# Layer 1's modulation blocks: scaled and added by GpSimd instead of multiplied by TensorE

## The chip, the cores and the metric

The kernel runs on one core of a Trainium2 chip. The time is device microseconds of one execution. A core has five engines with queues of their own: TensorE (PE; its weight loads are shown apart as PEld), VectorE (DVE), ScalarE (ACT), GpSimd (POOL) and SyncE (SP), which here only issues loads. SBUF is the on-chip memory; TensorE writes only to PSUM, which GpSimd does not touch here.

## The reference

Two models one after the other, on 256 tokens of width 1024. The change touches the first, which has two layers, and in them only the modulation ("adaln"): from a condition vector `c` each layer gets six vectors of 1024, which shift, scale and gate its two halves (mixer and experts).

```python
def adaln(cond, mod_w, mod_b):
    m = jax.nn.silu(cond) @ mod_w + mod_b        # (1024) @ (1024, 6144)
    return jnp.split(m, 6, axis=-1)
for i in range(2):
    sh1, sc1, g1, sh2, sc2, g2 = adaln(c, mod_w[i], mod_b[i])
    a = rms_norm(h, norm1_g[i]) * (1 + sc1) + sh1
    y = even_mixer(a, ...) if i == 0 else odd_mixer(a, ...)
    h = h + g1 * y
    h = h + g2 * hier_moe(modulate(h, norm2_g[i], sh2, sc2), ...)
```

Layer 0 also needs the first vectors of a second condition, `c_ctx`; layer 1 needs those of `c` alone. `hier_moe` routes each token to 2 of 16 experts, chosen within one of four groups. Everything is computed in float32.

## The kernel before

**Blocks.** A layer's modulation matrix is 24 MB, cut into 12 blocks of 512 output columns; a block is two loads of 1 MB (`chunk`, L125), each 128 partitions by four slices of 512. Block j of a layer gives columns 4j to 4j+3 of `mods[layer]` (48 columns of 128 values): 0 to 7 shift 1, 8 to 15 scale 1, 16 to 23 gate 1, 24 to 31 shift 2, 32 to 39 scale 2, 40 to 47 gate 2.

**How a block is computed.** The class `Conditions` (L357) does it on TensorE. `add` (L364) loads the two halves and multiplies each of the eight slices as the moving operand (128x512) with 32 columns of `cpad`, which holds silu(c) and silu(c_ctx) between zeros (L375); four slices stand in four strips of the array at one time, so the sum over partitions falls into four strips of one PSUM bank. `keep` copies the bank to SBUF on ScalarE (L384). `finish` multiplies the copy, in four pieces of 128 columns, with a selection matrix (L396), which adds the strips and turns the row into a column, and VectorE adds the bias (L399).

**Where the blocks stand.** The list `left` holds all 24 blocks in order, and `PLAN` (L58) says how many are taken at each of 17 places. Layer 0's are taken in its own mixer and do not concern the change. Layer 1's stand at four places:

- four (`PLAN[5]`) at the head of layer 0's experts (`moe`, L421), kept after the first gather and finished in step 1;
- two (`PLAN[16]`, the object `c3`, L1006) beside layer 1's value projection (`oin_v`);
- four (`PLAN[6]`, `more`, L404 and L1057) after the odd mixer's input projection, before its output projection;
- two (`PLAN[7]`) at the head of layer 1's experts.

**The experts' stage.** `moe` first computes the router on VectorE from the logits of the norm (L454 to L494): a chain of some thirty small instructions that ends in `selb`. TensorE then counts ranks (L483), VectorE makes one-hot matrices (`oh`, L513), and TensorE gathers the tokens of four experts (`gps`, L535) into `xg`. Eight steps follow (L748), two experts in each: `up` (L557), transposes (L571, L573), `down` (L590), and the scatter back (L599). The gather for the next four experts is made every second step (`prepare`). From step 2 the experts are taken in an order found at run time, so SP issues those loads (L717) only when VectorE has that order in memory. After step 7 stands a branch (L772) for experts with more than 64 tokens, which all engines take or skip; in this data it is taken once in layer 0 and skipped in layer 1.

**The odd mixer.** After a row norm, `oin_v` gives the value part (L1009), then eight chunks of the input projection (`feature_linear`, L201, called at L1039) follow, two for each of four parts, and four of the output projection (L1061). Each 1 MB chunk of these is split into two halves of 128x1024, and each half into a rounded part on ScalarE (`whi`, L133) and the remainder on VectorE (`wlo`, L134), with two buffers each; TensorE does three matmuls for each product. `Norm` (L228) begins, before the output projection, with matmuls on shift 2, and scale 2 goes into the gain it uses from the second chunk on.

**What sets the order.** Each engine runs its instructions in the order in which the program issues them, with small changes by the planner, and waits on semaphores. All 1 MB loads are issued by SP, in program order, each into the next of 13 buffers (three pools of 4, 7 and 2, `rings`, taken in turn); a load waits until what its buffer held has been used. So a load that waits holds up all loads behind it. PSUM has eight banks; tag "T" (`tps`) has two, one of which holds a fourth of the experts' result in that stage.

```python
T.matmul(self.ps[32 * k:32 * k + 32, :], cpad[:, 4 * h + k, 32 - 2 * at:64 - 2 * at],
         w[:, k, :], start=(at == 0 and h == 0), stop=(h == 1), tile_position=(0, 32 * k), ...)
```

Of the kernel before, what the change touches and what calls it, by code (L numbers as in the profile page):

```python
# [19 lines left out]
D = 1024  # L20
S = 256
# [31 lines left out]

GT = 9

FILL = (0, 0, 0, 1, 1, 2, 0, 2, 0)

PLAN = (1, 1, 1, 1, 2, 4, 4, 2, 1, 1, 0, 0, 0, 0, 0, 0, 2)  # L58


def build(tc, I, O):
# [3 lines left out]
    with es:  # L65
# [31 lines left out]
        def F(name):  # L97
            a, n = PF[name]
            return pf[:, a:a + n]
# [303 lines left out]

        def more(n, small):  # L404
            c = Conditions(small)
            c.add(n)
            c.finish()

# [11 lines left out]

        def moe(layer, norm, rc, work, blocks):  # L421
            small = work
            lg, shift = norm.lg, norm.router[1]
            cond = Conditions(work)
            cond.add(blocks)
            def t(n, name):
# [155 lines left out]
            def down(turned, dns, first, last):  # L582
                ht, back, cws = turned
                wd = [dns(e) for e in range(2)]
                yg = pair([128, D], "yg", small, bufs=2)
                for q in range(2):
# [37 lines left out]
            prepare(0)  # L624
            cond.keep()

# [121 lines left out]
            for step in range(9):  # L748
# [9 lines left out]
                if step < 8:  # L758
                    q, h_ = divmod(step, 2)
                    hs[step] = up(quarter[q][0], 128 * h_, lambda h, e: weights_of(step, h, e), turned)  # L760
                    if h_ == 0 and q < 3:
                        prepare(q + 1)
                    if step == 1:
                        rks, cws_, res = more_blocks()
                        cond.finish(kept=True)
                        V.tensor_copy(g2, mods[layer][:, 40:48, 0])
                else:
                    turned()
                    for e in range(2):
                        weights_of(7, 2, e)  # L770
                    over, rest = (value(intr, i, (EN.PE, EN.Activation, EN.DVE, EN.Pool), 8) for i in range(2))
                    with tc.If(over > 0):  # L772
                        overflow(res, cwp[:, :, 14:16], lambda h, e: weights_of(7, h, e), lambda e: weights_of(7, 2, e))
                        with tc.If(rest > 0):  # L774
                            overflow_any(0)
                            with tc.If(rest > 2):
                                for i in range(1, 4):
                                    overflow_any(i)
# [39 lines left out]
        with tc.tile_pool(name="l0", bufs=1) as wk:  # L818
# [158 lines left out]
            for cj in range(4):  # L977
# [3 lines left out]
                for mm in range(2):  # L981
                    m = 2 * cj + mm
                    residual(m, ps[:, S * mm:S * mm + S], mods[0][:, 16 + m:17 + m, 0])
                c2.add(PLAN[8 + cj])
            norm.add2(xT, 6)
            c2.finish()
            rc = norm.finish(after=AF.Exp, pool=c1)
        ring_m = b1.enter_context(tc.tile_pool(name="ring_m", bufs=2))
        rings[:] = [ring, ring_b, ring_b, ring_m, ring, ring_b, ring_b, ring, ring_b, ring_m, ring_b, ring, ring_b]
        with tc.tile_pool(name="m0", bufs=1) as wk:  # L990
            collect, norm = moe(0, norm, rc, wk, PLAN[5])
            for m in range(NK):
                collect(m)
                norm.add(xT, m)
            rx = norm.finish(c1)
# [4 lines left out]
        with tc.tile_pool(name="l1", bufs=1) as wk:  # L1000
# [4 lines left out]
            loaded["oin_v", 0] = chunk("oin_v", 0)  # L1005
            c3 = Conditions(wk, ops)  # L1006
            c3.add(PLAN[16])
            c3.keep()
            token_linear("oin_v", 0, (a,), lambda b, ps: A.copy(vt[:, b], ps.rearrange("p (g c) -> p g c", g=4)),  # L1009
                         need=step)  # L1010
            c3.finish(kept=True)
            vf = vt.rearrange("p b g c -> p (b g) c")
            sq = wk.tile([128, 8, 128], F32, name="vsq", tag="zc")
            A.activation(sq, vf, AF.Square)
# [6 lines left out]
            nc.scalar.dma_start(sgw, I["sg_w"])  # L1021
            sT = wk.tile([128, 4, S], F32, name="sT")
            for g in range(4):
# [10 lines left out]
            z = hx  # L1034
            zc = wk.tile([128, 4, S], F32, name="zc", tag="zc")
            cv = F("conv")
            for part in range(4):
                for cj in range(2):
                    ps = feature_linear("oin", 2 * part + cj, a)  # L1039
# [9 lines left out]
                    else:  # L1049
                        V.tensor_tensor(z[:, two], pv, hx[:, two], op=ALU.mult)  # L1050
                        for m in (2 * cj, 2 * cj + 1):
# [4 lines left out]
                                                   zc[:, m, 0:S - 1], op0=ALU.mult, op1=ALU.add)  # L1056
            more(PLAN[6], wk)  # L1057
            c2 = Conditions(wk, tps)
            norm = Norm(wk, None, router=(mod_gain(1, 4, 0, F("n2g")[:, 8:16], "G21"), mods[1][:, 24:32, 0], 1), tag=("mf", 2))
            for cj in range(4):  # L1060
# [3 lines left out]
                for mm in range(2):  # L1064
                    m = 2 * cj + mm
                    residual(m, ps[:, S * mm:S * mm + S], mods[1][:, 16 + m:17 + m, 0])
                c2.add(PLAN[12 + cj])
            norm.add2(xT, 6)
            c2.finish()
            rc = norm.finish(after=AF.Exp, pool=c1)  # L1070
        with tc.tile_pool(name="m1", bufs=1) as wk:
            collect, _ = moe(1, norm, rc, wk, PLAN[7])
        b1.close()
# [760 lines left out]
```

## Time and profile before

| | |
|---|---|
| Median of three runs | 1518.34 us (1518.15 to 1519.94) |
| Profiled execution | 1520.81 us, of which the span from first to last instruction is 1519.1 |
| TensorE busy | 1481.3 us, 98% of the span |
| VectorE busy | 858.3 us, 56% |
| ScalarE busy | 658.4 us, 43% |
| GpSimd busy | 28.5 us, 2%, 59 instructions |
| Mean granted TensorE clock | 0.981 of full speed |
| Data moved | 324.85 MB, 214 GB/s in the mean |

The first model fills some 615 us of the span: layer 0's mixer to about 170, its experts to 350, the odd mixer to 465, layer 1's experts to 617; the second model is not touched. A busy TensorE is not one at its peak, as matmuls are pipelined and their ends are modelled; the timeline tells more, where a row gives the start, the duration of a run of like instructions and, in brackets, the idle time before it with what ended that. The times in one execution differ from those of the median run by the 0.16% between 1520.81 and 1518.34.

### The profile page before, as it was taken

What the parts mean: (1) busy time and instruction counts of PE and PEld (TensorE: products, weight loads), DVE (VectorE), ACT (ScalarE), POOL (GpSimd) and SP (SyncE); (2) the same over time, 40 slices, a digit from 0 to 9 for tenths busy, and PEclk for the clock granted to TensorE, in tenths of its full rate; (3) what the DMA queues carried; (4) which work ended last, traced back from release to release, by engine and by line L of the source; (5) the groups of instructions that cost most, each with busy time, mean ns of one, the idle gap of its engine ahead of it and who ended that gap; (6) DMA issues with size and microseconds to landing.
All of it is one profiled execution on the core that took longest, in us unless ns stands there. A gap on an engine that the chain in (4) does not pass through costs nothing.

```text
span 1519.1 us, 25566 instructions
## 1 busy us (share of the span) xinstructions
PE 1481.3 (98%) x10410; PEld 1183.6 (78%) x10412; DVE 858.3 (56%) x1682; ACT 658.4 (43%) x1114; POOL 28.5 (2%) x59
## 2 busy tenths in 40 slices
PE   8999999989999999999999999999999999999998
PEld 3756644445985443698789999999898789999998
DVE  2775452225646221757777775555757777765554
ACT  2544311115433111565564554444564654654443
POOL 0000000000000000020000000000110000000000
PEclk9999899999999999999999999999999999999999
DMA  9974799739585985543315564554444134555540
GB/s 395 385 301 160 302 373 408 293 127 379 206 337 193 416 328 222 180 167 112 139 57 178 184 222 174 188 195 167 135 158 165 57 112 174 188 220 176 188 167 28
DMA packets 47005, 324.85 MB, mean 214 GB/s; under 512 B 5600, under 2 KB 5984, under 8 KB 8480
## 3 DMA queue, kind: packets, MB, share of 16 engines
q1 hardware_dynamic: 45360, 320.12, 55.4%
q8 instruction: 86, 1.41, 0.4%
q10 hardware_dynamic: 1296, 1.55, 0.3%
q0 software_dynamic: 224, 1.46, 0.3%
q14 instruction: 39, 0.32, 0.1%
HBM read 322.06 MB, written 1.05 MB: 213 GB/s over the span
## 4 chain that ended last, share of the span: by engine, by line
PE 55%; issue 3%; ACT 1%; DVE 1%; POOL 0%; DVEq 0%; POOLq 0%; ACTq 0%
PE fm L162 9%; PE fm L161 9%; PE fm L163 9%; PE d L162 4%; PE d L161 4%; PE d L163 4%; PE tm L194 1%; PE tm L196 1%; PE tm L195 1%; PE sp L1461 1%; PE lf L162 1%; PE lf L163 1%; PE lf L161 1%; PE po L1450 1%; PE ptp L1444 1%
## 5 line engine op out<-in xcount | busy, mean ns | idle before, releaser
L134 DVE TENSOR_TENSOR wlo<-w,whi 128x1024 fp32r<-128x1024 f32 (+1 forms) x314 | 378.4, 1208 | 254.2 <-ACT whi L133 251.6
L133 ACT CAST whi<-w 128x1024 fp32r<-128x1024 f32 (+1 forms) x314 | 324.4, 1035 | 393.6 <-PE fm L162 240.5
L161 PE MATMUL fm<-acth,whi 128*128 128x256 f32 x624 | 180.8, 290 | 0.0
L162 PE MATMUL fm<-actl,whi 128*128 128x256 f32 x624 | 179.9, 288 | 0.0
L163 PE MATMUL fm<-acth,wlo 128*128 128x256 f32 x624 | 179.1, 287 | 0.0
L163 PE MATMUL d<-hidh,wlo 128*128 128x256 f32 x512 | 144.2, 282 | 0.0
L162 PE MATMUL d<-hidl,whi 128*128 128x256 f32 x512 | 144.0, 281 | 0.0
L161 PE MATMUL d<-hidh,whi 128*128 128x256 f32 x512 | 143.9, 281 | 0.0
L162 PE MATMUL fm<-oTl,whi 128*128 128x256 f32 x512 | 143.6, 281 | 0.0
L163 PE MATMUL fm<-oTh,wlo 128*128 128x256 f32 x512 | 143.3, 280 | 0.0
L161 PE MATMUL fm<-oTh,whi 128*128 128x256 f32 x512 | 143.1, 280 | 0.0
L162 PEld LDWEIGHTS fm<-actl,whi 128*128 128x128 f32 x624 | 120.7, 193 | 3.2 <-issue 3.0
L163 PEld LDWEIGHTS fm<-acth,wlo 128*128 128x128 f32 x624 | 120.7, 193 | 2.2 <-issue 1.6
L161 PEld LDWEIGHTS fm<-acth,whi 128*128 128x128 f32 x624 | 121.4, 195 | 1.2 <-issue 0.8
L162 PEld LDWEIGHTS fm<-oTl,whi 128*128 128x128 f32 x512 | 96.8, 189 | 0.4 <-DVE oTl L1100 0.4
L162 PEld LDWEIGHTS d<-hidl,whi 128*128 128x128 f32 x512 | 96.7, 189 | 0.4 <-DVE hidl L134 0.4
L161 PEld LDWEIGHTS fm<-oTh,whi 128*128 128x128 f32 x512 | 96.9, 190 | 0.0
L161 PEld LDWEIGHTS d<-hidh,whi 128*128 128x128 f32 x512 | 96.8, 189 | 0.1
L163 PEld LDWEIGHTS d<-hidh,wlo 128*128 128x128 f32 x512 | 96.7, 189 | 0.1
L163 PEld LDWEIGHTS fm<-oTh,wlo 128*128 128x128 f32 x512 | 96.7, 189 | 0.0
L590 PE MATMUL yp<-w,ht 128*64 128x512 f32 x272 | 83.8, 643 | 6.9 <-PEq L774 3.5
L557 PE MATMUL gu<-w,xg 128*64 128x512 f32 x288 | 70.1, 599 | 0.0
(531 smaller groups left out, 2862.3 us busy)
## 6 DMA issues: line engine op xcount, KB each, us to landing
w<-gu SPq DMA_DIRECT2D x64, 1024.0 KB, 9.1
w<-mod SPq DMA_DIRECT2D x48, 1024.0 KB, 11.7
w<-dn SPq DMA_DIRECT2D x32, 1024.0 KB, 9.7
w<-gw SPq DMA_DIRECT2D x32, 1024.0 KB, 4.8
w<-up SPq DMA_DIRECT2D x32, 1024.0 KB, 4.8
w<-dw SPq DMA_DIRECT2D x32, 1024.0 KB, 4.8
w<-tm SPq DMA_DIRECT2D x12, 1024.0 KB, 4.8
w<-oin SPq DMA_DIRECT2D x8, 1024.0 KB, 8.2
```

The source lines that it names most:

```text
L133: A.copy(hi, src)
L134: V.tensor_sub(lo, src, hi.bitcast(F32))
L161: T.matmul(out, ws[0], xs[0], start=first, stop=False, skip_group_check=skip)
L162: T.matmul(out, ws[0], xs[1], start=False, stop=False, skip_group_check=skip)
L163: T.matmul(out, ws[1], xs[0], start=False, stop=last, skip_group_check=skip)
L194: T.matmul(ps, at[0], ww[0], start=first, stop=False, skip_group_check=True)
L195: T.matmul(ps, at[1], ww[0], start=False, stop=False, skip_group_check=True)
L196: T.matmul(ps, at[0], ww[1], start=False, stop=k == NK - 1, skip_group_check=True)
L557: T.matmul(gu[64 * e:64 * e + 64, :], x_[:, 4 * h + k, s0 + 64 * e:s0 + 64 * e + 64], w[e][:, 512 * k:512 * k + 512], start=(h == 0 and k ...
L590: T.matmul(yp[64 * e:64 * e + 64, :], ht[:, 128 * k + 64 * e:128 * k + 64 * e + 64], wd[e][:, 1024 * k + 512 * q:1024 * k + 512 * q + 512] ...
L1444: T.transpose(tp[:, 128 * c:128 * c + 128], prs[g][:, 128 * c:128 * c + 128], ident)
L1450: T.matmul(po[64 * g:64 * g + 64, 0:S], vals(g, 0), prs[g][:, 0:S], start=first, stop=False, tile_position=(0, 64 * g), skip_group_check=True)
```

## The change

Layer 1's twelve blocks leave TensorE's dense path. `Conditions` stays for layer 0. Two new functions take its place:

- `begin(n)` loads a block's two halves. On GpSimd, in place, it scales each of the eight slices by its column of silu(c) (one value per partition), adds the four slices of a half together, and the second half's sum to the first's, into a tile `sm` of 128x512. There are three such tiles (`SUMS`), in a pool `msums` that opens when layer 0's mixer closes and lies in memory that the mixer had.
- `end(n)` sums `sm` over its partitions: four matmuls with a 128x128 piece of `sm` as the stationary and one column of ones as the moving operand, into a PSUM tile of tag "T", and an addition of the bias on VectorE.

The blocks' places change: six are begun in steps 0 to 5 of layer 0's experts and ended in steps 2 to 7, after the step's `up`; four are begun in the odd mixer (two after the first chunk of the input projection, one after the second, one after the fourth) and ended after chunks 4, 6 and 8 and once more behind them; two are begun in steps 0 and 1 of layer 1's experts and ended in steps 3 and 4. Gate 2 is copied (`g2`) after step 7 instead of in step 1.

To make room, the pair `yg` has one buffer instead of two, and two tiles of the odd mixer (`vsq`, `zc`) share memory with others. `more`, `c3` and the second use of `c2` go; `PLAN` keeps layer 0's entries.

```diff
+SUMS = 3
+EXPERT_PLAN = ((1, 1, 1, 1, 1, 1, 0, 0), (1, 1, 0, 0, 0, 0, 0, 0))
+EXPERT_ENDS = ((0, 0, 1, 1, 1, 1, 1, 1), (0, 0, 0, 1, 1, 0, 0, 0))
+MIXER_PLAN = (2, 1, 0, 1, 0, 0, 0, 0)
+MIXER_ENDS = (0, 0, 0, 1, 0, 1, 0, 1)
-PLAN = (1, 1, 1, 1, 2, 4, 4, 2, 1, 1, 0, 0, 0, 0, 0, 0, 2)
+PLAN = (1, 1, 1, 1, 2, 1, 1)
...
-        def more(n, small):
...
+        sums, msums = [], []
+
+        def begin(n):
+
+            for _ in range(n):
+                layer, j = left.pop(0)
+                sm = msums[0].tile([128, 512], F32, name="msum", tag="msum", bufs=SUMS)
+                for h in range(2):
+                    w = chunk(f"mod{layer}", 2 * j + h).rearrange("p (k n) -> p k n", k=4)
+                    for k in range(4):
+                        G.tensor_scalar(w[:, k], w[:, k], cpad[:, 4 * h + k, 32:33], None, op0=ALU.mult)
+                    G.tensor_tensor(w[:, 0:2], w[:, 0:2], w[:, 2:4], op=ALU.add)
+                    if h:
+                        G.tensor_tensor(w[:, 0], w[:, 0], w[:, 1], op=ALU.add)
+                        G.tensor_tensor(sm, sm, w[:, 0], op=ALU.add)
+                    else:
+                        G.tensor_tensor(sm, w[:, 0], w[:, 1], op=ALU.add)
+                sums.append((layer, j, sm))
+
+        def end(n):
+
+            for _ in range(n):
+                layer, j, sm = sums.pop(0)
+                p2 = tps("m2")
+                for q in range(4):
+                    T.matmul(p2[:, q:q + 1], sm[:, 128 * q:128 * q + 128], ones[:, 0:1], start=True, stop=True)
+                V.tensor_tensor(mods[layer][:, 4 * j:4 * j + 4, 0], p2[:, 0:4],
+                                F(f"mod_b{layer}")[:, 4 * j:4 * j + 4], op=ALU.add)
...
-            cond = Conditions(work)
-            cond.add(blocks)
...
-                yg = pair([128, D], "yg", small, bufs=2)
+                yg = pair([128, D], "yg", small)
...
-            cond.keep()
...
                     if step == 1:
                         rks, cws_, res = more_blocks()
-                        cond.finish(kept=True)
-                        V.tensor_copy(g2, mods[layer][:, 40:48, 0])
+                    end(EXPERT_ENDS[layer][step])
+                    begin(EXPERT_PLAN[layer][step])
                 else:
                     turned()
                     for e in range(2):
                         weights_of(7, 2, e)
+                    V.tensor_copy(g2, mods[layer][:, 40:48, 0])
...
+        msums.append(b1.enter_context(tc.tile_pool(name="msums", bufs=1)))
...
-            c3 = Conditions(wk, ops)
-            c3.add(PLAN[16])
-            c3.keep()
...
-            c3.finish(kept=True)
...
+                    end(MIXER_ENDS[2 * part + cj])
+                    begin(MIXER_PLAN[2 * part + cj])
-            more(PLAN[6], wk)
-            c2 = Conditions(wk, tps)
+            end(1)
```

## Rows read from the trace of the kernel before

**Rows 1.** The page's first part: busy time, share of the span, instructions

```profile
PE 1481.3 (98%) x10410; PEld 1183.6 (78%) x10412; DVE 858.3 (56%) x1682; ACT 658.4 (43%) x1114; POOL 28.5 (2%) x59
```

**Rows 2.** Timeline, head of layer 0's experts: start, duration (us), engine, line, operation

```profile
166.20 0.50 PE L235 MATMUL nps<-cst,sqs 128*128 128x1 f32 x4
...
167.53 1.05 PE L375 MATMUL mps<-w,cpad 128*32 128x512 f32 x2
...
172.20 0.17 DVE L266 RECIPROCAL rc<-rs 128x2 f32<-128x2 f32 x1 [3.86 <-ACT rs L263]
...
176.23 6.88 PE L375 MATMUL mps<-w,cpad 128*32 128x512 f32 x48 [1.31 <-DMA w<-mod]
...
183.04 0.18 PE L483 MATMUL rank<-selb,strib 128*128 128x16 bf16 x1
...
190.08 1.08 PE L557 MATMUL gu<-w,xg 128*64 128x512 f32 x4
```

**Rows 3.** Timeline, head of layer 1's experts

```profile
462.50 1.07 PE L375 MATMUL mps<-w,cpad 128*32 128x512 f32 x8
...
465.06 0.17 DVE L266 RECIPROCAL rc<-rs 128x2 f32<-128x2 f32 x1 [3.74 <-ACT rs L263]
...
469.12 0.18 PE L483 MATMUL rank<-selb,strib 128*128 128x16 bf16 x1 [1.69 <-DVE selb L480]
...
476.56 1.08 PE L557 MATMUL gu<-w,xg 128*64 128x512 f32 x4
```

**Rows 4.** TensorE's timeline, odd mixer: value projection and end of input projection

```profile
373.14 1.06 PE L396 MATMUL m<-cst,ms 128*128 128x4 f32 x8
...
422.69 7.07 PE L375 MATMUL mps<-w,cpad 128*32 128x512 f32 x64
...
430.48 1.06 PE L396 MATMUL m<-cst,ms 128*128 128x8 f32 x8 [0.71 <-ACT ms L384]
...
431.95 1.86 PE L228 MATMUL nps<-rw,mod 128*128 128x20 f32 x16
```

**Rows 5.** Stretches: us, busy time and count of PE, PEld, DVE, ACT, POOL; PE clock; DMA

```profile
168.00:170.00 2.00, 2.00 (x12) 1.49 (x11) 0.35 (x2) 0.00 (x0) 0.00 (x0) 0.78 0.00 0
...
220.00:230.00 10.00, 10.00 (x56) 5.12 (x52) 3.55 (x9) 1.33 (x3) 0.00 (x0) 1.00 1.01 427
...
350.00:360.00 10.00, 9.04 (x44) 3.53 (x42) 6.42 (x10) 3.95 (x9) 0.00 (x0) 1.00 0.98 404
...
390.00:400.00 10.00, 10.00 (x86) 10.00 (x85) 4.76 (x5) 3.98 (x5) 0.00 (x0) 1.00 0.56 200
```

**Rows 6.** TensorE's timeline, layer 0's experts: last steps

```profile
302.62 7.09 PE L557 MATMUL gu<-w,ug 128*64 128x512 f32 x32
...
331.14 3.65 PE L590 MATMUL yp<-w,ht 128*64 128x512 f32 x16 [0.52 <-DVE ht L575]
...
340.88 6.47 PE L590 MATMUL yp<-w,ht 128*64 128x512 f32 x16 [3.54 <-PEq L774]
```

**Rows 7.** GpSimd, by line and in its timeline

```profile
L1228 POOL COPY dup<-zr 128x512 f32<-128x512 f32 x4 | 2.3, 611 | 53.8 <-DVE zr L1179 53.8
...
38.70 0.45 POOL L857 TENSOR_TENSOR turned<-cst,pb 128x128 f32<-128x128 f32 x1
...
39.11 0.60 POOL L860 TENSOR_TENSOR turned<-cst,pb 128x64 f32<-128x64 f32 x2
```

**Rows 8.** GpSimd alone (679 us), then GpSimd and VectorE at one time (721 us)

```profile
679.52 1.76 POOL L1383 TENSOR_TENSOR cblk<-qkT,pe 64x120 f32<-64x120 f32 x4 [20.17 <-ACT qkT L1239]
...
721.00 2.63 POOL L1383 TENSOR_TENSOR cblk<-vcT,pe 64x120 f32<-64x120 f32 x4 [39.71 <-ACT vcT L1371]
...
721.51 1.41 DVE L134 TENSOR_TENSOR wlo<-w,whi 128x1024 fp32r<-128x1024 f32 x1
```

**Rows 9.** ScalarE's and VectorE's timeline, one half of a weight chunk, odd mixer

```profile
411.17 1.05 ACT L133 CAST whi<-w 128x1024 fp32r<-128x1024 f32 x1 [1.79 <-PE fm L162]
...
412.25 1.22 DVE L134 TENSOR_TENSOR wlo<-w,whi 128x1024 fp32r<-128x1024 f32 x1 [0.27 <-ACT whi L133]
```

More of the change, by code (lines that the diff above doesn't have):

```diff
@@ L402, in finish @@
                 self.ps, self.blocks = None, []
-        def more(n, small):
-            c = Conditions(small)
-            c.add(n)
-            c.finish()
+        sums, msums = [], []
[22 more added lines that the diff above has]
+                                F(f"mod_b{layer}")[:, 4 * j:4 * j + 4], op=ALU.add)
         left = [(i, j) for i in range(2) for j in range(12)]
@@ L418, in residual, with moe @@
             V.scalar_tensor_tensor(xT[:, m], ps_ap, gate, xT[:, m], op0=ALU.mult, op1=ALU.add)
-        def moe(layer, norm, rc, work, blocks):
+        def moe(layer, norm, rc, work):
             small = work
             lg, shift = norm.lg, norm.router[1]
-            cond = Conditions(work)
-            cond.add(blocks)
             def t(n, name):
@@ L983, in build @@
                     residual(m, ps[:, S * mm:S * mm + S], mods[0][:, 16 + m:17 + m, 0])
-                c2.add(PLAN[8 + cj])
+                c2.add(PLAN[5 + cj] if cj < 2 else 0)
             norm.add2(xT, 6)
@@ L990, in build @@
         with tc.tile_pool(name="m0", bufs=1) as wk:
-            collect, norm = moe(0, norm, rc, wk, PLAN[5])
+            collect, norm = moe(0, norm, rc, wk)
             for m in range(NK):
@@ L1005, in build @@
             loaded["oin_v", 0] = chunk("oin_v", 0)
-            c3 = Conditions(wk, ops)
-            c3.add(PLAN[16])
-            c3.keep()
             token_linear("oin_v", 0, (a,), lambda b, ps: A.copy(vt[:, b], ps.rearrange("p (g c) -> p g c", g=4)),
                          need=step)
-            c3.finish(kept=True)
             vf = vt.rearrange("p b g c -> p (b g) c")
-            sq = wk.tile([128, 8, 128], F32, name="vsq", tag="zc")
+            sq = wk.tile([128, 8, 128], F32, name="vsq", tag="mixh")
             A.activation(sq, vf, AF.Square)
@@ L1021, in build @@
             nc.scalar.dma_start(sgw, I["sg_w"])
-            sT = wk.tile([128, 4, S], F32, name="sT")
+            sT = wk.tile([128, 4, S], F32, name="sT", tag="sT")
             for g in range(4):
@@ L1034, in build @@
             z = hx
-            zc = wk.tile([128, 4, S], F32, name="zc", tag="zc")
             cv = F("conv")
             for part in range(4):
+                if part == 2:
+                    zc = wk.tile([128, 4, S], F32, name="zc", tag="sT")
                 for cj in range(2):
@@ L1066, in build @@
                     residual(m, ps[:, S * mm:S * mm + S], mods[1][:, 16 + m:17 + m, 0])
-                c2.add(PLAN[12 + cj])
             norm.add2(xT, 6)
-            c2.finish()
             rc = norm.finish(after=AF.Exp, pool=c1)
         with tc.tile_pool(name="m1", bufs=1) as wk:
-            collect, _ = moe(1, norm, rc, wk, PLAN[7])
+            collect, _ = moe(1, norm, rc, wk)
         b1.close()
```

## The prediction

> **What bounds the kernel now.** I read four views, in this order. The page's first part: TensorE has work for 98% of the span and GpSimd for 2% [rows 1], so the change takes work from the engine that sets the end and gives it to one that stands still. Busy time alone doesn't tell what an instruction is worth, so next the timeline of TensorE at each place where a modulation block runs [rows 2 to 4], to see whether a wait lies under it. Then the clock and the DMA rate by stretch [rows 5] and the experts' last steps [rows 6], and last GpSimd and VectorE wherever both work [rows 7 to 9], because that overlap will become the rule. Three places matter: the head of layer 0's experts, the odd mixer, the head of layer 1's experts.
>
> The sum is a difference, made in the profiled execution (1520.81 us, span 1519.1, 1.7 around it) and laid on the median of the runs, 1518.34, which is 0.16% lower.
>
> **What is taken away.** A block is 16 matmul records (64 for four [rows 4]).
> - Head of layer 0's experts. Four blocks stand before the rank matmuls: from the reciprocal's end (172.37) to the first expert matmul (190.08) 17.7 us pass [rows 2]. In layer 1's head, where two blocks stand, it is 465.23 to 476.56, 11.3 us, and there the rank matmul waits for VectorE's selb, so the blocks lie under the router's chain [rows 3]. Taken: 6.4.
> - In both heads block matmuls also stand among the norm's own: 1.05 at 167.53 [rows 2], 1.07 at 462.50 [rows 3], on the chain to the reciprocal, less what one waits for anyway. Taken: 0.9 and 1.1.
> - End of the odd mixer. From 422.69 to 431.95 TensorE does the four blocks, waits for their copy, and turns them [rows 4]: 9.3 taken. ScalarE's copies are under that time and go with it.
> - The other three closings of layer 1 (experts 0, value projection, experts 1), 1.06 each [rows 4]: 3.2 taken.
> - The two blocks beside the value projection lie where TensorE waits for the norm (it has 9.04 of 10 us as busy, but 3.5 of weight loads [rows 5]): 0, at most 1.1.
>
> **What is added on TensorE.** Twelve ends of four narrow matmuls, eight records each, with a 128x128 stationary. The nearest rows are the closings, eight records in 1.06 [rows 4], and four 128x1 records in 0.50 [rows 2]. So 12.0 to 12.7; I take 12.7. Nothing hides them: they stand among dense matmuls. Net so far: -6.4 - 0.9 - 1.1 - 9.3 - 3.2 + 12.7 = -8.2.
>
> **The clock.** Around 169 us TensorE does only the sparse norm matmuls and its clock falls (0.78 over 168 to 170), while in 350 to 360, where blocks fill the norm's gaps, it stays at 1.00 [rows 5]. Without the fillers the second stretch is like the first, and the value projection starts at 1.2 GHz. What that costs is in the trace: 16 expert matmuls after the branch took 6.47, the same 16 before it 3.65 [rows 6]. So 0 to 2.8; I take 1.4, as VectorE feeds that stage slowly at first anyway.
>
> **GpSimd's own time.** A block is 8 scalings of 512, 2 additions of 1024, 3 of 512. Additions: 0.45 for 128 and 0.30 for 64 elements [rows 7] give 0.16 + 2.2 ns per element, so 1.27 and 2.4. A scaling isn't in the trace; it lies between the copy of 512, 0.61, and the addition, 1.27. With the copy a block is 4.9 + 4.8 + 3.8 = 13.5 us, with the addition 18.8. I take 13.5 (one tensor input, as the copy). A step of the experts is (302.62 - 190.08) / 7 = 16.1 us [rows 2, 6], and each sum is read two steps after it was begun, so neither value makes TensorE wait. In the mixer four blocks are 54 us; GpSimd is past the branch by 340.9 [rows 6], so they end near 395 to 400, before the reads (chunks 4, 6, 8 and the end, 397 to 423). The twelve small additions of the mods on VectorE wait behind TensorE with nothing queued that is urgent: 0. One buffer for `yg`, the shared tiles of the mixer and the later copy of gate 2 cost nothing by the order alone: TensorE issues a step's scatter, the last reader of `yg`, ahead of the matmuls that the next `yg` is made from.
>
> **GpSimd beside VectorE.** Here the bounds are wide. Four GpSimd additions take 1.76 alone and 2.63 with a VectorE subtraction among them; that subtraction of two SBUF tiles takes 1.41, against 1.22 [rows 8, 9]. So GpSimd loses 0.87 and VectorE 0.19, beside GpSimd instructions of 0.44; the new ones are up to 2.4. Where VectorE has slack this costs nothing (in steps 2 to 7 of the experts its inputs are mostly PSUM). It has little in two places.
> - The router's chain of layer 0. Its first sum may only be written once layer 0's mixer has left its memory, so GpSimd resumes about when the chain starts. Of the chain, some nine instructions read two SBUF tiles and have no other wait before them: 9 x 0.2 = 1.8; with a whole mean GpSimd instruction each (13.5 / 13 = 1.04) 9.4.
> - The weight halves of the mixer's projections. ScalarE's cast starts at 411.17, VectorE's remainder ends at 413.47 [rows 9]; TensorE's 24 matmuls of a half take 24 x 10 / 86 = 2.8 [rows 5], so it asks at about 414.0: slack 0.55. A wait of 0.2 fits in, so 0 by the nearest row. If a whole instruction is waited out, an arrival in a 2.4 us addition (35% of GpSimd's time) waits 1.2 on average, 0.65 too long, in a 1.27 us one (28%) 0.1 too long: 0.26 a half, over the 18 or so halves that GpSimd's six later blocks overlap, 4.6. I take 1.5, nearer to the row.
>
> Sum: -8.2 + 1.4 + 1.8 + 1.5 = -3.5; forecast 1514.8.
>
> The Trainium skill's "SBUF — State Buffer", § Who interferes with whom, speaks against the change: a VectorE instruction with two SBUF inputs and a GpSimd instruction that reads SBUF lock each other out, and whichever starts first keeps the shared port for its whole length. The rows of 721 us agree in kind, with short instructions. By it the two upper bounds stand: 9.4 and 4.6.
>
> **DMA.** The 24 loads of 1 MB stay, but layer 0's experts now load 12 in their steps, where 8 came ahead and 4 after. At 427 GB/s [rows 5] a load is 2.46 us; a step with a block is 8 loads, 19.7 us, against its 16.1. With 13 buffers full at the start, five more than a step takes (12 us), and six such steps short by 3.6 (22 us), up to 10 us would be missing at the end; but the two last steps load nothing new, and a step's weights are wanted only at its middle. I cost it at 0. SP gets the mixer's loads in another order (two before each next chunk), all earlier than wanted. The twelve loads are released by GpSimd, within 14 us of landing.
>
> **The rivals.**
> - GpSimd's long instructions hold VectorE up (ends slower). Place: the two above. Price: -8.2 + 2.8 + 9.4 + 4.6 = +8.6, so 1527. It decides from a mean wait of about 0.65 us: 9 x 0.65 + 18 x 0.1 = 7.7, and the gain is gone. For it: the 1.41, and instructions five times as long. Against: in those rows GpSimd gives way more than VectorE.
> - No cost beside the ends: -8.2 and half the clock, 1511.
> - Loads late: with the 10 us above, two thirds seen, 1521. For it: DMA share 1.01 in the experts [rows 5]. Against: TensorE never waits there for weights now.
> - A scaling far slower than a copy. From 22 us a block the sixth sum is late for the last step; at 2.5 us a scaling a block is 28.6, six end at 176 + 172 = 348, some 38 after the read: 1552. That would be the change not doing what it says, TensorE waiting for what it was spared.
>
> **How the numbers follow.** The forecast's case, 1511.5 to 1518, gets 0.38; no cost 0.20; VectorE held up 0.27; late loads 0.10; slow scaling 0.05. Range 1507 to 1530: it leaves out the slow scaling and the tails. About 0.2% (3 us) can be told from no change: below 1515.3 lie the second case and 0.6 of the first, 0.43; within, 0.24; above 1521.4, 0.33.
>
> **What would show it.** First expert matmul of layer 0 some 11 to 13 us after the reciprocal, not 17.7; if later, router instructions of VectorE longer than in [rows 2]'s stretch. About 5 us from the last input chunk to the output projection's norm matmuls. Eight-record ends of 1.06 without a wait for GpSimd. Remainders still 1.22, or up to 3.6. Clock at 0.5 near 360. Wrong if TensorE waits for a sum or for weights in the experts, or if the halves of the mixer take over 3 us.

## The result, and the profile after

The changed kernel takes 1543.17 us (median of four runs, 1540.72 to 1553.47), the kernel before 1518.55 on the same chip: a ratio of 1.0162, 95% interval 1.0141 to 1.0183. The forecast was 1514.8 with a range to 1530: wrong in sign and outside the range. The profiled execution took 1541.06, its span is 1539.4.

First the page: part 1, and from part 5 the costliest group of GpSimd (busy time, mean ns of one, then the idle time before it).

```profile
PE 1469.4 (95%) x10284; PEld 1189.3 (77%) x10284; DVE 897.0 (58%) x1690; ACT 656.5 (43%) x1110; POOL 304.9 (20%) x215
...
L420 POOL TENSOR_SCALAR w<-w,cpad 128x512 f32<-128x512 f32 x96 | 166.2, 1746 | 84.9 <-DMA w<-mod 84.9
```

TensorE lost 12 us of busy time against [rows 1] and the span grew by 20: the time went into waits. VectorE has 8 instructions more than before and 39 us more of busy time; a stretched instruction counts as busy, so most of this is waiting too (the eight are small additions). One scaling takes 1.75 us in the mean.

Where the span grew is read from TensorE's timeline, at the same instruction in both kernels (start; lag against before in brackets; the third column is the experiment `x1_no_gpsimd_math` below):

| | before | changed | GpSimd's arithmetic left out |
|---|---|---|---|
| first expert matmul, layer 0 | 190.08 | 190.00 (-0.1) | 182.09 (-8.0) |
| first down matmul, step 0 | 211.49 | 211.43 (-0.1) | 202.39 (-9.1) |
| down matmuls inside the branch | 331.14 | 346.16 (+15.0) | 337.13 (+6.0) |
| value projection | 360.66 | 372.40 (+11.7) | 363.07 (+2.4) |
| input projection | 374.47 | 391.41 (+16.9) | 375.97 (+1.5) |
| norm's matmuls on shift 2 | 431.95 | 452.61 (+20.7) | 428.61 (-3.3) |
| first expert matmul, layer 1 | 476.56 | 496.64 (+20.1) | 474.12 (-2.4) |
| span | 1519.1 | 1539.4 (+20.3) | 1517.0 (-2.1) |

The changed kernel's rows, which answer to [rows 2, 3, 4 and 6]:

```profile
190.00 1.98 PE L586 MATMUL gu<-w,xg 128*64 128x512 f32 x4
...
346.16 3.65 PE L619 MATMUL yp<-w,ht 128*64 128x512 f32 x16 [0.52 <-DVE ht L604]
...
372.40 0.73 PE L200 MATMUL tm<-whi,ah 128*128 128x512 f32 x2 [3.80 <-ACT ah L338]
...
387.13 0.80 PE L201 MATMUL tm<-whi,al 128*128 128x512 f32 x1 [3.92 <-DVE al L339]
...
391.41 0.38 PE L167 MATMUL fm<-ah,whi 128*128 128x256 f32 x1
...
449.88 1.84 PE L435 MATMUL m<-cst,msum 128*128 128x1 f32 x16
...
452.61 0.63 PE L234 MATMUL nps<-rw,mod 128*128 128x20 f32 x5
...
496.64 1.08 PE L586 MATMUL gu<-w,xg 128*64 128x512 f32 x4
```

**The head of layer 0's experts, all engines.** The blocks are gone from TensorE, yet the first expert matmul comes no sooner.

```profile
170.58 0.17 DVE L272 RECIPROCAL rc<-rs 128x2 f32<-128x2 f32 x1 [1.66 <-ACT rs L269]
...
175.04 2.34 POOL L421 TENSOR_TENSOR w<-w 128x1024 f32<-128x1024 f32 x1
175.31 2.12 DVE L509 SCALAR_TENSOR_TENSOR selb<-before,og 128x32 bf16<-128x32 f32 x1
177.46 1.30 POOL L423 TENSOR_TENSOR w<-w 128x512 f32<-128x512 f32 x1
...
177.55 1.26 DVE L519 TENSOR_TENSOR sel<-pr,selb 128x32 f32<-128x32 f32 x1
...
177.69 0.17 PE L512 MATMUL rank<-selb,strib 128*128 128x16 bf16 x1 [7.70 <-DVE off L517]
...
178.85 0.19 DVE L459 TENSOR_REDUCE om<-sel 128x2 f32<-128x32 f32 x1
...
180.41 0.76 PE L564 MATMUL gps<-oh,whi 128*128 128x256 f32 x2 [2.45 <-DVE oh L542]
```

Read each VectorE row beside the GpSimd row above it. `selb` reads two SBUF tiles of 32 columns; it starts 0.27 us after GpSimd's addition and ends at 177.43, 0.05 after the addition does (177.38). `sel` ends at 178.81, the addition beside it at 178.76. VectorE waits out what is left of the addition. The reduction `om` reads one tile and takes its usual 0.19, though the next addition began 0.12 before it. TensorE, idle before the ranks and again before the gather, pays. Its clock pays too: without the blocks it is granted 0.50 over 180 to 190, the lower of its two levels (0.83 in the kernel before), and the first four expert matmuls take 1.98, before 1.08 [rows 2].

**The mixer's weight halves, all engines.** It is the same with the remainder `wlo`: 1.22 alone [rows 9], 3.33 where it starts just after an addition of 1024 columns (its end, 410.77, is 1.1 behind the addition's).

```profile
407.28 2.40 POOL L421 TENSOR_TENSOR w<-w 128x1024 f32<-128x1024 f32 x1
407.44 3.33 DVE L140 TENSOR_TENSOR wlo<-w,whi 128x1024 fp32r<-128x1024 f32 x1 [0.32 <-ACT whi L139]
...
410.82 0.39 PE L169 MATMUL fm<-ah,wlo 128*128 128x256 f32 x1 [1.32 <-DVE wlo L140]
```

VectorE's remainders by line from the norm to the output projection: the changed kernel (364 to 455 us), then the kernel before (350 to 433).

```profile
L140 DVE TENSOR_TENSOR wlo<-w,whi 128x1024 fp32r<-128x1024 f32 x22 | 34.9, 1590 | 10.5 <-ACT whi L139 10.5
```

```profile
L134 DVE TENSOR_TENSOR wlo<-w,whi 128x1024 fp32r<-128x1024 f32 x22 | 26.8, 1223 | 15.3 <-ACT whi L133 13.6 <-DMA w<-mod 1.5
```

**GpSimd with VectorE nearly idle**, its timeline in the experts' steps. Four scalings take 6.18, 1.55 each; the additions take what was forecast from [rows 7], 2.4 and 1.27.

```profile
212.18 6.18 POOL L420 TENSOR_SCALAR w<-w,cpad 128x512 f32<-128x512 f32 x4 [28.08 <-DMA w<-mod]
218.44 2.36 POOL L421 TENSOR_TENSOR w<-w 128x1024 f32<-128x1024 f32 x1
220.87 1.26 POOL L426 TENSOR_TENSOR msum<-w 128x512 f32<-128x512 f32 x1
```

The next block begins at 233.81, so a block is 21.6 us, against steps of 16.

**The loads and the steps**, by stretches with the columns of [rows 5] (DMA share and GB/s last): first changed, then before.

```profile
180.00:190.00 10.00, 6.79 (x25) 5.57 (x25) 9.04 (x22) 0.47 (x1) 4.10 (x3) 0.50 0.31 107
190.00:200.00 10.00, 10.00 (x45) 4.02 (x45) 8.44 (x44) 3.04 (x5) 0.00 (x0) 0.88 0.30 106
...
250.00:260.00 10.00, 9.71 (x43) 4.87 (x44) 1.66 (x3) 1.38 (x2) 9.84 (x7) 0.83 1.01 426
```

```profile
180.00:190.00 10.00, 8.49 (x61) 5.25 (x53) 5.82 (x23) 1.06 (x2) 0.00 (x0) 0.83 1.00 422
190.00:200.00 10.00, 10.00 (x55) 4.74 (x54) 9.19 (x44) 3.00 (x5) 0.00 (x0) 1.00 0.61 227
```

Before, TensorE emptied eight buffers by 183 us and transfers ran at 422 GB/s. Changed, all buffers are full of weights that wait for the first step, and transfers fall to 107. Later they run near full. But no wait of TensorE in the steps ends with a load. It stands at three places, each time before transposes (`htp`) and again before the end of a block right behind them. The first, in TensorE's timeline:

```profile
247.41 0.41 PE L600 MATMUL htp<-cst,hh 128*128 128x128 f32 x2 [0.67 <-DVE hh L594]
...
249.31 1.02 PE L435 MATMUL m<-cst,msum 128*128 128x1 f32 x8 [1.27 <-DVE cws L608]
250.26 5.37 PE L619 MATMUL yp<-w,ht 128*64 128x512 f32 x16
```

The end takes a PSUM tile of tag "T", as the transposes do, and waits until VectorE has read them (`cws` is the last read). The other two places have 0.93 and 1.27, so the six waits make 6.4 us. (The second 1.27 is put down to GpSimd's sum `msum`; with the arithmetic left out it is as long and ends with `cws`.) Behind two of the three the granted clock is lower (0.83 over 250 to 260), and 16 down matmuls take 5.37 and 5.40, elsewhere 3.65: 3.5 more.

### The profile page after: what moved, and what is told of

Read it like the earlier page. It is cut to its first block, busy times and chain, and to the rows that moved or that the text cites. A ratio compares the mean times of both kernels' runs of the same rounds, so it can differ in the third digit from the quotient of the medians.

```text
span 1539.4 us, 25489 instructions
## 1 busy us (share of the span) xinstructions
PE 1469.4 (95%) x10284; PEld 1189.3 (77%) x10284; DVE 897.0 (58%) x1690; ACT 656.5 (43%) x1110; POOL 304.9 (20%) x215
## 3 DMA queue, kind: packets, MB, share of 16 engines
q10 hardware_dynamic: 1296, 1.55, 0.3%
HBM read 322.06 MB, written 1.05 MB: 210 GB/s over the span
## 4 chain that ended last, share of the span: by engine, by line
PE 54%; issue 3%; ACT 1%; DVE 1%; POOL 0%; DVEq 0%; POOLq 0%; ACTq 0%
PE fm L168 9%; PE fm L169 9%; PE fm L167 9%; PE d L168 4%; PE d L167 4%; PE d L169 4%; PE tm L200 1%; PE tm L202 1%; PE tm L201 1%; PE sp L1487 1%; PE lf L168 1%; PE lf L169 1%; PE lf L167 1%; PE ptp L1470 1%; PE po L1476 1%
## 5 line engine op out<-in xcount | busy, mean ns | idle before, releaser
L140 DVE TENSOR_TENSOR wlo<-w,whi 128x1024 fp32r<-128x1024 f32 (+1 forms) x314 | 389.5, 1243 | 244.9 <-ACT whi L139 243.9
L420 POOL TENSOR_SCALAR w<-w,cpad 128x512 f32<-128x512 f32 x96 | 166.2, 1746 | 84.9 <-DMA w<-mod 84.9
```

The lines of the kernel that those rows point to most:

```text
L140: V.tensor_sub(lo, src, hi.bitcast(F32))
L420: G.tensor_scalar(w[:, k], w[:, k], cpad[:, 4 * h + k, 32:33], None, op0=ALU.mult)
```

## Experiments

Ratios are to the kernel before, in runs on the same chip; times "at" are from a run's own profile. Line numbers are each kernel's own.

**Four that take the change apart.** GpSimd's arithmetic left out:

```diff
-                    for k in range(4):
-                        G.tensor_scalar(w[:, k], w[:, k], cpad[:, 4 * h + k, 32:33], None, op0=ALU.mult)
-                    G.tensor_tensor(w[:, 0:2], w[:, 0:2], w[:, 2:4], op=ALU.add)
...
+                    G.tensor_copy(sm[:, 256 * h:256 * h + 256], w[:, 0:256])
```

> GpSimd's scalings and additions of layer 1's blocks are left out; it copies 256 columns of each half into the sum, so layer 1's modulation is not computed. Loads and ends stay. Two causes (GpSimd's additions hold VectorE; the loads come late): the 20 us that the head of layer 0's experts, the value and the input projection lost (7 + 5 + 8) come back, but from the first expert matmul to the last regular down matmuls it stays near 156 us (before 141), for the loads are the same: 1523. Rival A (GpSimd, 21 us a block, holds the load buffers and so delays the loads): these 156 fall to 146 too, 1513. Rival B (only the places of the ends among TensorE's work matter): 1540.

Measured 1519.49, ratio 0.9992 (0.9980 to 1.0005). TensorE's timeline:

```profile
182.09 1.08 PE L579 MATMUL gu<-w,xg 128*64 128x512 f32 x4
...
337.13 2.37 PE L612 MATMUL yp<-w,ht 128*64 128x512 f32 x10 [0.52 <-DVE ht L597]
...
428.61 1.66 PE L234 MATMUL nps<-rw,mod 128*128 128x20 f32 x11
```

The head is 8 us shorter, the remainders are back at 1.23, but from 182.09 to 337.13 it is still 155.0, before 141.1. From the down matmuls of step 0 to those in the branch it is 134.7 in both kernels (before 119.7), with the same six waits: the arithmetic costs nothing there. In all it costs 22.4 us of span (1539.4 - 1517.0; 26 by the two ratios), and with the arithmetic free the change would gain nothing that can be told from no change. Rival B is out for the whole, and of rival A nothing is seen in this length.

The six blocks of layer 0's experts from a resident tile, no loads:

```diff
+                    if layer == 1 and j < 6:
+                        w = still[0].rearrange("p (k n) -> p k n", k=2)   # one load of 128x1024, once
```

> The six blocks of layer 0's experts are worked out by GpSimd from one resident tile of 128x1024 in place of twelve loads, so they are not layer 1's modulation. Same GpSimd instructions, same ends. Two causes: from the first expert matmul to the last regular down matmuls 146 us instead of 156, VectorE still held in the head and the mixer: 1533. Rival A (held buffers): the same here. Rival B (places of the ends): stays at 156, 1543.

Measured 1536.06, ratio 1.0111 (1.0080 to 1.0142). TensorE's timeline, then that of all engines:

```profile
183.45 1.12 PE L593 MATMUL gu<-w,xg 128*64 128x512 f32 x2
...
212.22 1.03 PE L626 MATMUL yp<-w,ht 128*64 128x512 f32 x4
...
336.34 1.94 PE L626 MATMUL yp<-w,ht 128*64 128x512 f32 x8 [0.52 <-DVE ht L611]
```

```profile
193.03 2.17 POOL L428 TENSOR_TENSOR still<-still 128x1024 f32<-128x1024 f32 x1
...
193.37 1.85 DVE L711 COPY ov<-cnt 128x4 f32<-128x4 f32 x1
```

152.9 where 146 was expected, but the excess lies before the first down matmuls (28.8, before 21.4): GpSimd began its first block only at 176.84 here and held VectorE in the chains that find the order of the experts and those with more than 64 tokens, where even a copy of four columns shows it. From the down matmuls of step 0 on it is 124.1, against 134.7 in the changed kernel and 119.7 before. The six ends there, 5.9 of busy time, cover the 4.4 over the kernel before. The 10.6 to the changed kernel are the six waits and the lower clock behind them, 9.9 together, and both are gone here, because TensorE's matmuls come in another order. TensorE's timeline, at the same place:

```profile
246.49 1.05 PE L442 MATMUL m<-cst,msum 128*128 128x1 f32 x8
247.47 3.65 PE L626 MATMUL yp<-w,ht 128*64 128x512 f32 x16
```

The changed kernel and the runs that only alter GpSimd's arithmetic share one order of the 624 matmuls in this stretch, with transposes and an end ahead of the next step's `up`. Without the twelve loads the planner leaves them behind its first matmuls, as in the kernel before. So the loads cost 10.6 by way of that order. What they would cost in the other order is not shown: no run has the loads with it.

Scalings alone (additions replaced by copies of 256 columns), and additions alone (the line `G.tensor_scalar` taken out):

> GpSimd's additions are left out (the scalings stay, and a copy of 256 columns for each half), so the blocks are not summed. Two causes, with the additions as the ones that hold VectorE: its waits in the router's chain of layer 0 fall from 7.8 us to under 3, and those of the two projections by half or more: 1529. Rival C (any GpSimd work at the same time slows VectorE in proportion to its time; scalings are 12.4 of a block's 21.3 us): 58% of the 20 us stays, 1534.

> GpSimd's scalings are left out, the additions stay, so the blocks are sums without their weights. Two causes, additions as the ones that hold VectorE: most of the 20 us stays, though GpSimd works 9 us a block, not 21: 1538. Rival C (in proportion to GpSimd's time): 42% stays, 1531.

Measured 1522.35, ratio 1.0010 (0.9993 to 1.0028), under both expectations, and 1558.9, ratio 1.0246 (1.0215 to 1.0276). The second has other modulations, so its tokens go to other experts and layer 1 takes the branch too (288 down matmuls, not 272). At layer 1's first expert matmul it is level with the changed kernel (496.15 and 496.64), and its span is 19.6 longer. Without these it would be 1539, an estimate, where 1538 was expected. The first expert matmul and the norm's matmuls on shift 2, scalings alone:

```profile
183.12 1.12 PE L581 MATMUL gu<-w,xg 128*64 128x512 f32 x2
...
438.00 1.86 PE L234 MATMUL nps<-rw,mod 128*128 128x20 f32 x16
```

With scalings the first expert matmul comes 1.0 later than without arithmetic, and the two projections take 13.6 and 52.9 us, against 12.9 and 52.6 without arithmetic and 19.0 and 61.2 changed; with additions 20.5 and 58.7. The additions hold VectorE, the scalings hardly: rival C is out. But the branch's down matmuls come at 345.14 with scalings alone, 8.0 later than without arithmetic, and there the changed kernel, 7 us later at the head, is only 1.0 behind. This looks like rival A, loads delayed by buffers that GpSimd holds while it scales. The trace does not bear it out: 6.4 of the 8.0 lie behind the same six waits, none of them longer. TensorE's timeline, scalings alone, at the first place:

```profile
241.87 1.43 PE L430 MATMUL m<-cst,msum 128*128 128x1 f32 x8 [1.27 <-DVE cws L603]
243.23 6.61 PE L614 MATMUL yp<-w,ht 128*64 128x512 f32 x16
```

The down matmuls behind the three places take 6.61, 6.63 and 6.10 here, without arithmetic 5.37, 3.70 and 5.40, and the ends 1.4 to 1.8 for 1.02: the clock was low for longer. Why is open. In the steps the lower clock thus takes 3 to 10 us, not always the same, and it hides 6 of the 7 us that the head of this run is ahead.

**One addition, or its length?** Every addition cut into pieces of 128 columns:

```diff
+                        for c in range(0, 512, 128):
+                            G.tensor_tensor(o[:, c:c + 128], a[:, c:c + 128], b[:, c:c + 128], op=ALU.add)
```

> The changed kernel with every addition of GpSimd cut into pieces of 128 columns, 28 for a block instead of 5, 0.44 us each: the same sums, and GpSimd works longer, some 25 us a block instead of 21. If VectorE waits for the end of the addition that runs, its wait is at most 0.44 us now instead of up to 2.4: about a quarter of the 23 us stays, 1526. Rival C (it loses in proportion to GpSimd's time): 1545 or more.

Measured 1551.17, ratio 1.0206 (1.0187 to 1.0225): far from 1526. All engines in the head, then TensorE at the end of the mixer:

```profile
182.33 0.48 DVE L667 TENSOR_TENSOR two<-two,top 128x2 f32<-128x2 f32 x1
182.33 1.70 POOL L423 TENSOR_TENSOR msum<-w 128x128 f32<-128x128 f32 x4
182.73 0.50 DVE L700 SCALAR_TENSOR_TENSOR ov<-cn,ov 128x16 f32<-128x16 f32 x1
183.16 0.49 DVE L668 SCALAR_TENSOR_TENSOR dd<-cst,two 128x16 f32<-128x16 f32 x1
```

```profile
451.00 1.86 PE L439 MATMUL m<-cst,msum 128*128 128x1 f32 x8 [16.55 <-POOL msum L423]
```

The wait did what was expected: VectorE's small instructions take turns with the pieces at some 0.49 each, the first expert matmul comes at 183.46, and the value projection takes 13.5. But GpSimd, now slower (24.1 a block), delivers the mixer's last sum late and TensorE waits 16.55 for it; without that wait it would be 1534.6, an estimate. The number is rival C's (1545 or more), the reason is not: it is the late sum of the forecast's last rival, met by mending something else.

**Another engine.** VectorE does the arithmetic in the changed kernel's plan (eight instructions a block):

```diff
-                        G.tensor_scalar(w[:, k], w[:, k], cpad[:, 4 * h + k, 32:33], None, op0=ALU.mult)
...
+                            V.scalar_tensor_tensor(sm, w[:, k], cpad[:, 4 * h + k, 32:33], sm, op0=ALU.mult, op1=ALU.add)
```

> The changed kernel with one thing replaced: VectorE works the blocks out, eight instructions of 128x512 for each (a scaling, then seven that scale and add in one; the same kind with 128x512 takes 0.73 us in the head), some 5.7 us a block, no GpSimd; loads, places and ends as in the changed kernel. If GpSimd's additions were what held VectorE, the loss in the head, value and input projection goes and the loads' loss stays: 1522 (1519 to 1528). Rival D (VectorE has no room for 68 us more, whoever makes it wait): 1535.

Measured 1540.12, ratio 1.0136 (1.0119 to 1.0153): rival D. The instructions take 0.745 us, about what was expected, but now stand in VectorE's own queue in the same places. Eight lie between the reciprocal and `selb`, and TensorE waits longer for the ranks than beside GpSimd (10.40, there 7.70). Two of the ends in the steps wait 2.9 instead of 1.27.

```profile
180.09 0.17 PE L509 MATMUL rank<-selb,strib 128*128 128x16 bf16 x1 [10.40 <-DVE selb L506]
```

**Other places.** Two moves from the kernel before, by VectorE: the mixer's four blocks into the last steps of layer 0's experts (`fetch`, `fold`, `end`), and the head's four into layer 0's mixer, in place.

```diff
-            more(PLAN[6], wk)
+FETCHES = (0, 0, 0, 0, 0, 1, 2, 1)
+FOLDS = (0, 0, 0, 0, 0, 0, 1, 2, 1)
...
             for cj in range(4):
+                fold(1, place=True)
                 ps = feature_linear("eout", cj, mix)
```

> The kernel before, with the four blocks of the end of the odd mixer moved: loaded after steps 5 to 7 of layer 0's experts, scaled and added by VectorE in steps 6, 7 and ahead of the branch, one ended in step 7 and three beside the value projection. Loads are put where the transfers stand still (310 to 340 us). The end of the mixer gives 9.3, the ends cost 1 to 4, the loads 0 to 3: 1513. Rival E (eight more loads cost 10 us wherever they are put in this stage): 1521.

> The kernel before, with the four blocks of the head of layer 0's experts scaled and added by VectorE, in place, before and during the output projection of layer 0's mixer; their four ends stand ahead of the router's ranks. The head gives 6.4 to 8.0: 1511. Rival F (VectorE's 23 us more among the halves of the mixer's weights delay them by as much): 1519.

> Both moves of the two kernels that run beside this one: four blocks early by VectorE in layer 0's mixer, four late in its experts, two each on TensorE at the value projection and in layer 1's head as before. If the two gains are independent: 1506; if the loads bound both: 1514.

Measured 1532.85, ratio 1.0082 (1.0065 to 1.0099); 1521.3, 0.9998 (0.9986 to 1.0010); 1532.04, 1.0080 (1.0063 to 1.0096). All missed. The end of the mixer did give its 9.3 (input projection to shift 2 48.1, before 57.5), but the blocks just ahead of the branch held up VectorE's one-hot matrices. TensorE's timeline and the stretch after it, late move alone:

```profile
329.10 1.94 PE L569 MATMUL gps<-oh,whi 128*128 128x128 f32 x8 [5.97 <-DVE oh L547]
```

```profile
330.00:340.00 10.00, 10.00 (x43) 7.22 (x44) 1.40 (x4) 1.48 (x4) 0.00 (x0) 0.57 0.40 166
```

After that wait the clock stood near 1.2 GHz (0.57), and the step lost 14 in all. Spread to one block a step, and the output projection's loads ahead of half the blocks':

```diff
+FETCHES = (0, 0, 0, 1, 1, 1, 1, 0)
+FOLDS = (0, 0, 0, 0, 1, 1, 1, 1)
```

> The kernel with both moves, with two mends: the late blocks one a step (scaled and added by VectorE after the up matmuls of steps 4 to 7, ended in steps 6 and 7 and twice behind the value projection), where two in a row held VectorE's answer to TensorE and TensorE's clock fell; and in layer 0's mixer the output projection's four loads stand ahead of half of the blocks' loads. If the waits at step 7 (15 us) and at the value projection (3 us) were what ate the gains: 1508. If the gains are not there: 1520 or more.

> The late move alone, one block a step. The end of the mixer gives 9.3, four ends cost 4.2, the loads 0 to 5 in steps 3 to 6: 1515. Rival E (eight more loads cost 10 us wherever they are put in this stage): 1525.

> The early move alone, the output projection's loads ahead of half of the blocks' loads. The head gives 6.4 to 8.0 and nothing is late in the output projection: 1513. Rival F (VectorE's 23 us more delay the halves): 1520.

> The late move alone, but scaled and added by GpSimd with the instructions of the changed kernel (21 us a block). If GpSimd's additions cost only where VectorE works on two SBUF tiles under TensorE's eyes (router, projections) and not in the experts' steps: as with VectorE, within 3 us, 1517. If they cost wherever they run: some 86 us of GpSimd work at the changed kernel's rate (23 us lost in 305 us of it), 6 more, 1521.

Measured 1518.2, ratio 0.9982 (0.9970 to 0.9994); 1518.09, 0.9989 (0.9978 to 1.0000); 1520.41, 0.9994 (0.9983 to 1.0005); 1518.27, 0.9987 (0.9971 to 1.0004). The late move is the same with GpSimd as with VectorE, as expected, though a block takes GpSimd 21 us: that fits steps in which TensorE seldom waits for VectorE work on two SBUF tiles, but no run isolates it. Rival E is out: with eight more loads in these steps the stretch to the branch is 123.4 (before 119.7), two ends among it, and TensorE stands at none of the three places. The others fall short of what was expected of them; the spread mended the step ahead of the branch, not the head. A delay that eats at the early move is seen on VectorE in the kernel with both: the bias addition of an end waits for TensorE's narrow matmuls, and the router's reciprocal is queued behind it.

```profile
177.06 0.16 DVE L440 TENSOR_TENSOR mod<-m,pf 128x4 f32<-128x4 f32 x1 [3.22 <-PE m L439]
...
177.34 0.16 DVE L272 RECIPROCAL rc<-rs 128x2 f32<-128x2 f32 x1
```

So the ends were moved: `end(4)` behind the first gather, the last two into the input projection.

> The kernel with both moves spread, and its ends moved off the chains that VectorE starts: the four early ones behind the first gather instead of ahead of the ranks (the reciprocal stood behind the bias additions at 177.3 us, 172.2 before), the two last ones in the input projection. If the place of the ends was what ate the early move: 5 to 7 less than that kernel's 1518, 1512. If not: 1518.

> The late move alone with its two last ends in the input projection instead of ahead of the value projection, where the norm to projection took 13.1 us, 11.6 before: 1516.5 instead of 1518. If the two blocks that TensorE keeps there and not the ends set that time: 1518.

Measured 1517.57, ratio 0.9981 (0.9964 to 0.9998), and 1518.86, ratio 0.9989 (0.9980 to 0.9998); 1512 was expected of the first and, if the ends mattered, 1516.5 of the second. The reciprocal is early now, but the ends run at the lower clock (two in 3.55, elsewhere 1.84) before the first expert matmul (186.52):

```profile
170.95 0.17 DVE L272 RECIPROCAL rc<-rs 128x2 f32<-128x2 f32 x1 [2.07 <-ACT rs L269]
...
175.43 3.55 PE L439 MATMUL m<-cst,w 128*128 128x1 f32 x16
```

The place of the ends shows in the trace (the reciprocal 6 us sooner), but the medians do not tell it, so what ate the early move is not settled. The spread kernels lie 0.1 to 0.2% below the kernel before, the edge of what can be told (three of the intervals reach 1.0000 or more), and no version found does better.

## Why the prediction was wrong, point by point

- *Taken from TensorE.* Right where nothing else hid it. The head gives 8.0 with the arithmetic out (forecast 7.3), the end of the mixer its 9.3.
- *GpSimd beside VectorE*, the step that failed most. It took the wait as 0.2 us from rows with instructions of 0.44 [rows 8], nearer "to the row". The wait is as long as what is left of the addition: up to 1.9 in the head. In span the arithmetic costs 22.4 instead of the 3.3 counted (1.8 + 1.5): some 9 up to the first down matmuls, nothing in the steps, 6.1 in the value projection, 8.6 in the input projection, less small differences behind them. The first rival had the mechanism and both places; its price, 9.4 + 4.6, was still too small, as the value projection was in neither of its places and the mixer's blocks ran longer.
- *Twelve ends at 1.06*, the second step that failed. Their size is right (0.95 to 1.05 in the trace), but "they stand among dense matmuls" is not so for three of the six in layer 0's steps: TensorE stands 6.4 us before them and the transposes ahead of them, and the lower clock behind costs 3.5. The sum had no term for either. "Nothing queued that is urgent" behind their additions held in the changed kernel and failed in the later ones that put ends on the router's chain.
- *GpSimd's own time.* The scaling is the term that was mis-sized: 1.55 alone, 0.61 taken, outside both bounds. A block is 21.6, not 13.5, and up to 26.8 in the input projection, so GpSimd ran on to 440 us in the mixer, not 395 to 400, and held VectorE all along that projection. The premise of the last rival, a slow scaling, came true, its late sum did not: the sixth sum was ready at 297.5, its end came at 314.94.
- *DMA, costed at 0.* Without the twelve loads the steps are 10.6 shorter, which is the 10 that the forecast worked out and argued away. The agreement is luck as far as the traces tell: TensorE waits for no load, and the time goes by the order of its matmuls, as above. The full buffers at the start (107 GB/s at 180 to 200 us), which the forecast counted as a help, are no wait of TensorE either.
- *Clock.* Right in kind: the value projection begins at the lower level (0.83 over 370 to 380, before 1.00; its first matmuls take 0.63, later ones 0.39). Without arithmetic that costs some 1.6 us, where 1.4 was taken. The norm ahead of it became 1.8 shorter without its two blocks (9.8, before 11.6), where 0 was taken. The further falls, in the head, in the steps and behind VectorE's waits, were in no term. (The 3.65 that the forecast compares with 6.47 belongs to the branch's own matmuls, another 16 of the same form.)
- The sum: -3.5 forecast in the span's terms, +20.3 found. Without contention -6.8 was forecast and -2.1 found: 4.7, the 9.9 of the waits and the clock in the steps less gains at the norm and in the head. Contention is the other 19.1 (22.4 - 3.3).

The Trainium skill's "SBUF — State Buffer", § Who interferes with whom, cited in the forecast, states that a VectorE instruction with two SBUF inputs, or a copy in a mode that takes both ports, and a GpSimd instruction that reads SBUF lock each other out of a shared port pair. The trace agrees for additions (2.12 beside 2.34), and for a copy by 1.85 beside 2.17, if that copy ran in such a mode, which no row tells. For the scalings it does not show it: VectorE's waits beside them were at most some 0.5 of their 1.55.

## What to carry to other kernels

An engine that stands still is not free if it shares a way to memory with one on the critical chain: price the wait by the length of the helper's longest instruction times the instructions of the chain, not by a share of busy time. Before work is taken off the busiest engine, ask what else it did there: here it filled the time of the router's chain, after which the clock is 0.83 over 180 to 190 with it and 0.50 without. Look, too, at what the moved instructions stand next to in the new order: an end of 1.0 us behind transposes costs its wait for their PSUM tile and, after it, some of the clock. A block's price on the new engine is to be measured for its own operation; bounds from two neighbours did not hold it.

## What was not expected of the hardware

- A GpSimd scaling of 128x512 by one value per partition takes 1.55 us, more than the addition of two tiles (1.27) and 2.5 times the copy (0.61). Why is open. The Trainium skill's "GPSIMD Engine Reference", § 4.1 Engine selection, has one-input operations roughly at line rate; the measurement decides.
- The scalings in their turn grow where VectorE works: four took 6.18 alone and up to 8.93 in the input projection. VectorE lost little to them: some 0.9 us in the router's chain (4.41 from the reciprocal to `before`, 3.56 without arithmetic).
- A copy of four columns on VectorE waited 1.7 us for a GpSimd addition; the comparison of two SBUF tiles that makes `oh` began 0.02 us ahead of an addition and did not wait (0.41).
- TensorE's clock after the same wait differs from run to run: behind a wait of 1.27 us, 16 down matmuls took 3.70 in one place and 6.63 in another.
